# The last tile in two activations and two multiplies of 4 rows instead of four of 2

## The chip, the cores and the metric

The kernel runs on one core of a Trainium2 chip. The metric is the device time of one execution in microseconds (us). Where a profile is shown, its times count from the start of the span, which is some 2 us shorter than the device time (468.5 us in the profile of a run of 470.59).

## The reference, cut to what matters

```python
def reference(x):                     # x: (32, 512, 2048) float32
    x1, x2 = x[..., :1024], x[..., 1024:]
    return (x1 * (1 / (1 + np.exp(-x1)))) * x2      # silu(x1) * x2
```

The input is 134 MB, the output 67 MB. Each element is used once.

## The kernel before

The 16,384 rows are cut into 16 tiles of 128 partitions x 8 rows. There are two input and two output buffers. For each tile ScalarE (ACT) writes silu of the first half into the output buffer, and VectorE (DVE) multiplies it in place by the second half. Loads are issued from SyncE's queue, stores from ScalarE's. `silu` and `mul` below take a range of rows.

```python
    load(0)
    load(1)
    for i in range(n_tiles):
        ...
        if i < n_tiles - 1:
            kc = KC_EDGE if i == 0 else K           # 2 rows at a time in tile 0, else all 8
            for c in range(0, K, kc):
                silu(ot, xt, c, c + kc)
                mul(ot, xt, c, c + kc)
            for ps, ks in OPENING if i == 0 else [(slice(None), slice(None))]:
                nc.scalar.dma_start(out=ov[ps, ks], in_=ot[ps, ks])
            if i + 2 < n_tiles:
                load(i + 2)
            continue
        # the last tile
        for c in range(0, K, KC_EDGE):              # KC_EDGE = 2
            silu(ot, xt, c, c + KC_EDGE)
            if c == K - KC_EDGE:
                nc.scalar.dma_start(out=ov[:, :KS], in_=ot[:, :KS])    # KS = 4
            mul(ot, xt, c, c + KC_EDGE)
        nc.scalar.dma_start(out=ov[:, KS:], in_=ot[:, KS:])
```

## Time and profile before

| | before |
|---|---|
| time, first three runs | 470.60, 470.62, 472.49 us |
| span of the profiled run | 468.5 us |
| DVE busy, ACT busy | 30%, 24% |
| traffic | 201.3 MB, 430 GB/s over the span |
| last tile's work released | 447.89 us |
| its two stores issued | 454.36 and 458.76 us |
| landed | 462.4 and 467.5 us |

The way to read it is from the end. The last row sets the span. Whether the rows above it matter depends on whether the transfer queue had other bytes to move when each store was issued. The lines are shown with the prediction.

### The profile page before, as it was taken

What the parts mean: (1) busy time and instruction counts of PE and PEld (TensorE: products, weight loads), DVE (VectorE), ACT (ScalarE), POOL (GpSimd) and SP (SyncE); (2) the same over time, 40 slices, a digit from 0 to 9 for tenths busy, and PEclk for the clock granted to TensorE, in tenths of its full rate; (3) what the DMA queues carried; (4) which work ended last, traced back from release to release, by engine and by line L of the source; (5) the groups of instructions that cost most, each with busy time, mean ns of one, the idle gap of its engine ahead of it and who ended that gap; (6) DMA issues with size and microseconds to landing.
All of it is one profiled execution on the core that took longest, in us unless ns stands there. A gap on an engine that the chain in (4) does not pass through costs nothing.

```text
span 468.5 us, 189 instructions
## 1 busy us (share of the span) xinstructions
DVE 139.5 (30%) x22; ACT 114.3 (24%) x23; POOL 0.2 (0%) x4
## 2 busy tenths in 40 slices
DVE  0070600704207052070510606116060150602551
ACT  1142305005050140601406023060230603206060
POOL 0000000000000000000000000000000000000000
DMA  9999999999999999999999999899999899999998
GB/s 425 397 453 425 448 403 403 492 403 403 448 487 408 403 448 414 481 403 425 425 448 448 403 448 492 358 448 448 431 464 448 380 425 492 403 448 403 448 403 359
DMA packets 4881, 201.34 MB, mean 430 GB/s; under 512 B 592, under 2 KB 592, under 8 KB 592
## 3 DMA queue, kind: packets, MB, share of 16 engines
q1 hardware_dynamic: 2304, 134.22, 66.4%
q10 hardware_dynamic: 2576, 67.11, 33.2%
q14 instruction: 1, 0.01, 0.0%
HBM read 134.22 MB, written 67.11 MB: 430 GB/s over the span
## 4 chain that ended last, share of the span: by engine, by line
DMA 72%; DVE 14%; ACT 11%; DVEq 0%; issue 0%
DMA out_dram<-ot 63%; DVE ot L93 14%; ACT ot L86 11%; DMA xt<-in_x_dram 9%; DVEq L148 0%
## 5 line engine op out<-in xcount | busy, mean ns | idle before, releaser
L93 DVE TENSOR_TENSOR ot<-ot,xt 128x8192 f32<-128x8192 f32 (+1 forms) x22 | 139.5, 6363 | 319.2 <-ACT ot L86 319.2
L86 ACT ACTIVATE ot<-xt 128x8192 f32<-128x8192 f32 (+1 forms) x22 | 113.0, 5163 | 340.1 <-DMA out_dram<-ot 306.1
L86 ACT ACT_TABLE_LOAD x1 | 1.3, 1283 | 0.8 <-PEq L137 0.8
L137 POOL MEMSET const-bfloat16-1.0<- 128x1 bf16 x1 | 0.1, 103 | 0.0
L137 POOL MEMSET const-uint8-127<- 128x1 uint8 x1 | 0.1, 102 | 0.0
L137 POOL MEMSET const-float32-0.0<- 128x1 f32 x1 | 0.1, 100 | 0.2 <-issue 0.2
L137 POOL MEMSET const-float32-1.0<- 128x1 f32 x1 | 0.1, 99 | 0.0
## 6 DMA issues: line engine op xcount, KB each, us to landing
out_dram<-ot ACTq DMA_DIRECT2D x14, 4096.0 KB, 42.2
out_dram<-ot ACTq DMA_DIRECT2D x3, 2048.0 KB, 8.8
out_dram<-ot ACTq DMA_DIRECT2D x2, 512.0 KB, 17.1
out_dram<-ot ACTq DMA_DIRECT2D x1, 768.0 KB, 27.9
xt<-in_x_dram SPq DMA_DIRECT2D x16, 35.1
out_dram<-ot ACTq DMA_DIRECT2D x1, 256.0 KB, 10.8
```

What stands on the lines that cost most here:

```text
L86: nc.scalar.activation(out=ot[:, c:ce, :], in_=xt[:, c:ce, :half], func=mybir.ActivationFunctionType.Silu,)
L93: nc.vector.tensor_mul(out=ot[:, c:ce, :], in0=ot[:, c:ce, :], in1=xt[:, c:ce, half:],)
L137: nc = _bacc.Bacc("TRN2", target_bir_lowering=False, num_devices=1)
```

## The change

The intent is fewer instructions in the last tile, each with its fixed cost, and both stores issued after all of its compute instructions. The first tile's five growing stores, which the change's description also names, are in both kernels.

```diff
-        for c in range(0, K, KC_EDGE):
-            silu(ot, xt, c, c + KC_EDGE)
-            if c == K - KC_EDGE:
-                nc.scalar.dma_start(out=ov[:, :KS], in_=ot[:, :KS])
-            mul(ot, xt, c, c + KC_EDGE)
-        nc.scalar.dma_start(out=ov[:, KS:], in_=ot[:, KS:])
+        for c in range(0, K, KS):
+            silu(ot, xt, c, c + KS)
+            mul(ot, xt, c, c + KS)
+        for c in range(0, K, KS):
+            nc.scalar.dma_start(out=ov[:, c:c + KS], in_=ot[:, c:c + KS])
```

## The prediction

> **What bounds the kernel now.** I read the page first (busy shares, the row of slices, traffic), then the chain of waits in order of time, the timeline of the tail, the instruction groups by form, and last the transfers in short windows of the tail. From the page:
>
> ```profile
> DVE 139.5 (30%) x22; ACT 114.3 (24%) x23; POOL 0.2 (0%) x4
> ...
> DMA  9999999999999999999999999899999899999998
> ...
> HBM read 134.22 MB, written 67.11 MB: 430 GB/s over the span
> ```
>
> Both compute engines are idle for 70% of the span or more; the transfer engines are at nine tenths in nearly every slice. The kernel is bound by 201.3 MB of traffic, and the change leaves every byte of it. So only the tail can matter: what the end waits for once the last bytes cannot be kept queued. The last lines of the chain of waits (start, us, what):
>
> ```profile
> 410.49 37.38 DMA out_dram<-ot
> 447.87 0.02 issue
> 447.89 1.92 ACT ot L86
> 449.81 0.02 issue
> 449.83 6.70 DVE ot L93 x3
> 456.53 2.20 DVEq L148
> ```
>
> The reader should see that the last tile's first activation (447.89) is released not by its input but by the landing of the store of two tiles earlier, which frees the output buffer. The last line is misleading: the chain ends at 458.73 with the last multiply, yet the span is 468.5 us. The last 9.8 us, a store, are missing from it. So I take the end from transfers, not from this chain. The timeline of the tail (start, us, engine, line; ACTq rows are store issues):
>
> ```profile
> 439.47 0.34 ACTq L112 DMA_DIRECT2D out_dram<-ot  x1
> 447.89 7.31 ACT L86 ACTIVATE ot<-xt 128x2048 f32<-128x2048 f32 x4 [17.17 <-DMA out_dram<-ot]
> 449.83 8.90 DVE L93 TENSOR_TENSOR ot<-ot,xt 128x2048 f32<-128x2048 f32 x4 [10.39 <-ACT ot L86]
> 454.36 0.34 ACTq L120 DMA_DIRECT2D out_dram<-ot  x1
> 458.76 0.34 ACTq L122 DMA_DIRECT2D out_dram<-ot  x1
> ```
>
> The list of issues in narrow windows around these three gives their times to landing: 18.0, 8.0 and 8.8 us. They land therefore at 439.47 + 18.0 = 457.5, 454.36 + 8.0 = 462.4 and 458.76 + 8.8 = 467.5. The spacing is the argument: from 447.87 (the landing before them) to 457.5 is 9.6 us for 4 MiB, then 4.9 and 5.1 us for 2 MiB each, all between 410 and 437 GB/s. The store queue never runs dry after 447.9. It drains 8 MiB at the full rate, while the last tile is computed beside it. When do the first bytes of the last tile begin? In the window from 456.8 to 457.2 the transfer view has
>
> ```profile
> DMA packets 32, 0.26 MB, mean 656 GB/s; under 512 B 16, under 2 KB 16, under 8 KB 16
> ```
>
> which I read as sixteen tiny packets, the end marks of the previous store, one for each transfer engine, and sixteen data packets of 16 KiB (16 x 16,384 B = 0.26 MB), each engine's first of the last tile. So the first half, issued at 454.36, waits some 2.4 to 2.8 us behind older bytes. The window 461.65 to 462.1 shows the same count for the second half: issued at 458.76, it waits about 3 us. These two slacks are all that the change can eat.
>
> **What the Trainium skill says.** "DMA: Bandwidth & Descriptors", section "Queues, rings and completion order", says that each transfer engine takes the descriptors of one issuing queue in ring order; the handover at 457.0 agrees, with the new store's packets beginning beside the old one's end marks. The same page, "Latency and other measured facts", gives about 600 ns from issue to first byte for transfers issued as here. The trace has one issue into empty queues, the opening load at 0.00 us, and its first packets begin later than that: the windows from 0.5 to 2 us show no traffic before 1.0 and 1835 GB/s from 1.0 to 1.5. I use the trace's 1.0 to about 1.8 us, though as the first transfer of the program it may be slower than a later one. [...]
>
> **The change part by part.** The mean durations come from the groups by form:
>
> ```profile
> L93 DVE TENSOR_TENSOR ot<-ot,xt 128x8192 f32<-128x8192 f32 x14 | 121.7, 8693 | 285.0 <-ACT ot L86 285.0
> L86 ACT ACTIVATE ot<-xt 128x8192 f32<-128x8192 f32 x14 | 98.4, 7029 | 303.1 <-DMA out_dram<-ot 288.9 <-DMA xt<-in_x_dram 14.2
> L93 DVE TENSOR_TENSOR ot<-ot,xt 128x2048 f32<-128x2048 f32 x8 | 17.8, 2286 | 34.2 <-ACT ot L86 34.2
> L86 ACT ACTIVATE ot<-xt 128x2048 f32<-128x2048 f32 x8 | 14.6, 1897 | 37.0 <-DMA xt<-in_x_dram 19.8 <-DMA out_dram<-ot 17.2
> ```
>
> *Activations.* The slope is (7029 - 1897)/6144 = 0.835 ns per element, so one of 4096 takes 1897 + 2048 x 0.835 = 3.61 us. Two replace four: busy 7.2 against 7.6 us. They still begin at 447.89, since what frees the buffer is untouched.
>
> *Multiplies.* The slope is (8693 - 2286)/6144 = 1.043, so 4.42 us each; two for four is 8.84 against 9.14 us busy. Back to back they start 0.08 us early into each other in the trace (four take 8.90 us of wall time).
>
> *Pipeline fill.* This is the cost. The first multiply can begin only after 3.61 us of activation instead of 1.90, so 1.71 us later: 447.89 + 3.61 + 0.04 = 451.54. It ends at 455.96. The second activation ends at about 455.1, before that, so the second multiply follows directly and ends at 455.96 - 0.08 + 4.42 = 460.30.
>
> *Stores.* They keep their size and split, two of 2048 KB. Placing the first issue after both activations costs nothing, since it waits for the multiply anyway. They are issued at about 455.98 and 460.33 instead of 454.36 and 458.76: 1.6 us later each. The saved fixed costs (1.71 late at the start, 1.57 at the end) return only 0.14 us.
>
> *Does the delay reach the end?* First half: issue 455.98, plus 1.0 to 1.4 us for most engines by the opening load, gives first bytes at 457.0 to 457.4, the last perhaps 457.8. The old store's bytes end between 456.8 and 457.2. Engine by engine that is a gap of 0 to 0.6 us, about 0.2 us on average; with the skill's 0.6 us it would be none. Second half: issue 460.33, first bytes 461.3 to 462.1; the first half, itself 4.9 us of transfer, ends at about 461.9 to 462.5. No second gap. Of 1.6 us of delay, some 1.4 are thus absorbed by the queue, and the sum is +0.2 us, rounded, on 470.62: 470.8 us.
>
> **The rivals.** *The queue runs dry.* If issuing takes longer than in the opening, say 2.0 us, the first half starts a full 1 us late and the time is about 471.6. If nothing were hidden at all it would be 470.62 + 1.6 = 472.2, the most that the delay can cost. For it: the margin is under 1 us, and landings, not first bytes, end the program. Against it: the measured slack of 2.4 to 2.8 us. *Fewer instructions win.* The saved 0.4 us of activation and 0.3 us of multiply could show if compute set the end; the chain of waits, which ends in DVE, seems to say so. That would give 470.0 at best. Against it: the pipeline fill costs more than the saving, and the last 9.8 us hold no compute. *All hidden anyway.* With a latency under 0.9 us the transfers do not move, and the time stays at 470.6. This is the nearest rival, and I cannot exclude it from one opening load.
>
> **Range and chances.** The before runs are 470.60, 470.62 and 472.49, so one run in three lies 0.4% up without any change; I let the range reach 472.1 for this and for most of the dry queue, and down to 470.3 for ordinary scatter. Two per cent is 9.4 us, six times the largest delay, so I give 98% to within 2%, and 1% each to faster and slower.
>
> **What would show it.** Right: groups of 128x4096 at about 3.61 and 4.42 us; the first multiply at 451.5; issues at 456.0 and 460.3; time to landing of both halves shortened by about 1.4 us, to 6.6 and 7.4; landings within 0.3 us of 462.4 and 467.5; the transfer row at full rate across 457. Wrong: a hole of over 0.6 us in the transfers after 457, or the stores' time to landing unchanged at 8.0 and 8.8 (the delay passed on whole), or any movement before 447.9.

## The result, and the profile after

| | before | changed |
|---|---|---|
| median of 6 runs each | 471.23 us (470.60 to 472.49) | 470.35 us (470.27 to 471.34) |
| ratio | | 0.9981, 95% interval 0.9964 to 0.9999: the same |

A ratio is the mean time of one kernel's fast runs over that of the other's in the same rounds, so it is not quite the ratio of the medians quoted. The before runs fall in two groups, three at 470.6 to 470.8 and three at 471.6 to 472.5, and the median of six lies between them. This makes the first difference look larger than it is; the controls below put it at 0.2 us.

The page of the changed kernel answers the first lines shown of before:

```profile
DVE 139.3 (30%) x20; ACT 114.1 (24%) x21; POOL 0.2 (0%) x4
...
HBM read 134.22 MB, written 67.11 MB: 430 GB/s over the span
```

Two instructions are gone from each engine, 0.2 us of busy time each; traffic and rate are the same. The new forms in the groups by form (busy us, then mean ns, then idle before):

```profile
L93 DVE TENSOR_TENSOR ot<-ot,xt 128x4096 f32<-128x4096 f32 x2 | 8.8, 4422 | 12.1 <-ACT ot L86 12.1
L86 ACT ACTIVATE ot<-xt 128x4096 f32<-128x4096 f32 x2 | 7.1, 3608 | 17.2 <-DMA out_dram<-ot 17.2
```

The timeline of the tail (start, us, engine, line):

```profile
439.57 0.34 ACTq L112 DMA_DIRECT2D out_dram<-ot  x1
448.01 7.12 ACT L86 ACTIVATE ot<-xt 128x4096 f32<-128x4096 f32 x2 [17.20 <-DMA out_dram<-ot]
451.66 8.76 DVE L93 TENSOR_TENSOR ot<-ot,xt 128x4096 f32<-128x4096 f32 x2 [12.13 <-ACT ot L86]
456.12 4.67 ACTq L120 DMA_DIRECT2D out_dram<-ot  x2
```

The last row merges the two store issues; the second starts at 456.12 + 4.67 - 0.34 = 460.45. The list of issues gives 6.4 and 6.9 us to landing, so they land at 462.5 and 467.4. The stores are issued 1.7 to 1.8 us later than before and land within 0.1 us of the same times: the delay was taken out of their wait in the queue. In the transfer view of 456.8 to 457.3 us the handover from tile 14's store is where it was, with all sixteen end marks and each engine's first 16 KiB of the last tile:

```profile
DMA packets 32, 0.26 MB, mean 524 GB/s; under 512 B 16, under 2 KB 16, under 8 KB 16
```

The chain of waits again ends in VectorE, with the last multiply:

```profile
448.01 3.62 ACT ot L86
451.64 0.02 issue
451.66 4.42 DVE ot L93
456.09 4.34 DVEq L146
```

That chain now ends at 460.43, 1.7 us later than the 458.73 of before, yet the span is not longer. So this end of the chain is no measure of the end of the program.

To compare tails, I count from the release of the last tile (its first activation's start) to the last landing: 467.51 - 447.89 = 19.62 us before and 467.38 - 448.01 = 19.36 us after (landings from the trace's records). The tail is 0.26 us shorter. Merging work that begins later should not do this, and the experiments look for it. One line differs in the transfer view. Between 463 and 464.2 us, inside its last store, the kernel before has

```profile
q10 hardware_dynamic: 30, 0.49, 96.0%
q14 instruction: 1, 0.01, 1.6%
```

(queue, kind, packets, MB, share of the 16 engines), one fetch of instructions, 8,192 B and 0.31 us on one transfer engine. The changed kernel has no instruction packet between the release and the last landing; the only one after the release stands in the trace at 469.02, after the end of the span (the kernel before has a second one there too, at 470.33). From 447.9 to 468 us its transfer view lists one queue:

```profile
q10 hardware_dynamic: 416, 7.86, 91.4%
```

The landings tell the same. A store lands in 16 parts, one for each transfer engine. In the kernel before, fifteen parts of the last store had landed 19.36 us after the release, no later than all sixteen of the changed kernel, and one came 0.26 us after them. The records don't say which engine the fetch ran on.

### The profile page after: what moved, and what is told of

It is laid out like the page before. It is cut to its first block, busy times and chain, and to the rows that moved or that the text cites. A ratio compares the mean times of both kernels' runs of the same rounds, so it can differ in the third digit from the quotient of the medians.

```text
span 468.4 us, 185 instructions
## 1 busy us (share of the span) xinstructions
DVE 139.3 (30%) x20; ACT 114.1 (24%) x21; POOL 0.2 (0%) x4
## 4 chain that ended last, share of the span: by engine, by line
DMA 72%; DVE 14%; ACT 11%; DVEq 1%; issue 0%
DMA out_dram<-ot 63%; DVE ot L93 14%; ACT ot L86 11%; DMA xt<-in_x_dram 9%; DVEq L146 1%
## 5 line engine op out<-in xcount | busy, mean ns | idle before, releaser
L93 DVE TENSOR_TENSOR ot<-ot,xt 128x8192 f32<-128x8192 f32 (+2 forms) x20 | 139.3, 6983 | 321.1 <-ACT ot L86 321.1
L86 ACT ACTIVATE ot<-xt 128x8192 f32<-128x8192 f32 (+2 forms) x20 | 112.8, 5661 | 340.2 <-DMA out_dram<-ot 305.8
```

The source lines that it names most:

```text
L86: nc.scalar.activation(out=ot[:, c:ce, :], in_=xt[:, c:ce, :half], func=mybir.ActivationFunctionType.Silu,)
L93: nc.vector.tensor_mul(out=ot[:, c:ce, :], in0=ot[:, c:ce, :], in1=xt[:, c:ce, half:],)
```

## The experiments

Two theories are to be told apart, for two different things. For the 1.7 us that vanished, **queue**: a store's delay costs nothing until its first bytes would come after the last bytes of the store ahead of it, and from there costs its full length. The rival is **compute**: the last multiply sets the end. For the 0.26 us that was won, **fetch**: the instruction fetch of 0.31 us fell out of the last store. The rival is that the merged tail itself gains, or that it is chance. Twelve kernels ran, all correct, each timed in 5 rounds beside the kernel before. Kernels of one set share its rounds: the first four, the next four and the last four. The sets ran on three different chips, where the kernel before had medians of 470.52, 470.58 and 470.64 us, so a tenth between sets says nothing. The edits are shown shortened, and are against the changed kernel unless said otherwise.

**1. The kernel before again** (no edit).

> The kernel before, unedited, as a control. It tells whether the difference of 0.19% (ratio 0.9981) is in the kernels or in the sample. Chance theory: its ratio to before lies in the same few tenths of a per cent, with an interval that holds 1. Fetch theory (an instruction fetch of 8 KB and 0.31 us fell into the last store of the kernel before at 463.6 us, and not into that of the changed kernel): the instruction row of the DMA queues shows one packet inside the span again and the last landing is again about 0.3 us later, counted from the release of the last tile, than in the changed kernel.

470.52 us median (470.35 to 471.57), ratio 0.9998 (0.9985 to 1.0012); the kernel before had 470.52 over 9 runs in these rounds. The profile fell on the run of 471.57. In it the last tile was released at 449.23 instead of 447.89, so the 1.3 us of that slower run arose upstream of everything that the change touches. The trace's end marks of tile 14's store show one transfer engine 1.2 us or more behind the fastest (456.82 to 458.51, against 456.83 to 457.17 in the first profile). The fetch was there again, at 464.86, but the tail was 19.36 us long. The expected 0.3 us did not show: the engine that was already behind set the end. The last parts of its three stores landed at 458.87, 463.76 and 468.60, 4.89 and 4.84 us apart; so the fetch did not delay that engine, and the other fifteen were done 1.0 us before it.

**2. The changed kernel again** (no edit).

> The changed kernel, unedited, as the other control. Queue theory: the same end, 0 to 0.3 us from before, ratio 0.9985 to 1.0005. Fetch theory: ratio 0.9993 or below (0.3 us or more faster), and no instruction packet within the last store. Compute theory (the last multiply sets the end): 1.6 us slower, ratio 1.003, which the first result already speaks against.

470.31 us median, all five runs within 470.29 to 470.44; ratio 0.9991 (0.9978 to 1.0003). The tail was 19.33 us and no fetch lay in it. The gain is 0.2 us against the median of before, and the interval still holds 1. The compute theory's 1.6 us is excluded.

**3. Only the multiplies merged.**

```diff
-            silu(ot, xt, c, c + KS)      # c = 0, 4
+            silu(ot, xt, c, c + 2)
+            silu(ot, xt, c + 2, c + 4)
             mul(ot, xt, c, c + KS)
```

> Only the multiplies of the last tile are merged (four activations of 2 rows, two multiplies of 4). The first multiply starts after two activations, about 3.7 us after the release, so the stores are issued some 1.6 us later than before, as in the changed kernel. Queue theory: nothing at the end, 470.2 to 470.7 us. Compute theory: +1.6 us. Fetch theory: if the fetch belongs to VectorE's instructions it vanishes here as in the changed kernel; if to ScalarE's it stays and the time is that of before.

**4. Only the activations merged.**

```diff
             silu(ot, xt, c, c + KS)      # c = 0, 4
-            mul(ot, xt, c, c + KS)
+            mul(ot, xt, c, c + 2)
+            mul(ot, xt, c + 2, c + 4)
```

> Only the activations of the last tile are merged (two activations of 4 rows, four multiplies of 2). The first multiply starts 1.7 us later than before, stores at about 456.0 and 460.4. Queue theory: nothing at the end, 470.2 to 470.7 us. Compute theory: +1.6 us. Fetch theory: if the fetch belongs to ScalarE's instructions it vanishes here as in the changed kernel; if to VectorE's it stays and the time is that of before.

470.94 us (470.90 to 471.04) and 471.04 us (470.92 to 471.29), both above the range that I gave the queue theory, and both slower than the fully merged tail (at most 470.44) in the same rounds. Yet their stores are issued at the same moments: 456.10 and 456.13 against 456.12 in the first profile of the changed kernel, and their first halves land at 462.5. Only the second half is late, with 7.5 us to landing in both instead of 6.9. In both, the transfer view from 462.6 to 468.5 us has the fetch, at 465.9 in the trace:

```profile
q14 instruction: 1, 0.01, 0.3%
```

So merging either half alone did not remove the fetch. At first this speaks against a fetch that belongs to one engine, for each kernel shares one engine's compute instructions with the changed one. The number of records may resolve it (a record is any instruction, wait or store issue that the trace lists for an engine). ScalarE's queue has 66 records in the kernel before, 64 in the changed one, and 66 in *both* of these: in kernel 3 because it keeps four activations, in kernel 4 because each of its two stores has come to wait on ScalarE as well as VectorE, which adds two waits. VectorE has 58 in kernel 3 and 60 in kernel 4. The number that goes with the fetch is ScalarE's. A second packet goes with VectorE's in the same way: all five profiles with 60 VectorE records, and none of the eight with 58, have one 1.8 us after the end of the span, where it delays nothing.

**5. Pieces of one row** (eight activations and eight multiplies, same stores).

```diff
-        for c in range(0, K, KS):
-            silu(ot, xt, c, c + KS)
-            mul(ot, xt, c, c + KS)
+        for c in range(K):
+            silu(ot, xt, c, c + 1)
+            mul(ot, xt, c, c + 1)
```

> The last tile in activations and multiplies of 1 row, same two stores. Fill is shorter: first store issued at about 453.6 us, some 0.8 us earlier than before and 2.4 us earlier than the changed kernel. Queue theory: no gain, since the first half still waits for the older bytes until about 457.0: 470.2 to 470.7 us, with times to landing longer by what the issue is earlier. Compute theory: the last multiply ends at about 458 us, so about 0.7 us faster than before.

471.47 us median, but from 470.25 to 472.51: too scattered to time a few tenths. Its profile is of a run released late, at 449.32. The first store was issued 5.75 us after the release, against 6.47 before and 8.11 changed; its first half took 8.8 us to landing; and the tail was 19.38 us. With issues up to 2.4 us apart, the tails are 19.38 here, 19.36 in the control of before and 19.36 and 19.33 in the changed kernel: issuing earlier gains nothing.

**6 to 8. The first activation made longer**: 5 and 3 rows, 6 and 2, and one of 8, with multiplies of 4 as in the changed kernel.

```diff
-        for c in range(0, K, KS):
-            silu(ot, xt, c, c + KS)
-            mul(ot, xt, c, c + KS)
+        silu(ot, xt, 0, 5)               # 6 in the next kernel, 8 (and no second) in the last
+        mul(ot, xt, 0, 4)
+        silu(ot, xt, 5, 8)
+        mul(ot, xt, 4, 8)
```

> The changed kernel with activations of 5 and 3 rows instead of 4 and 4. Activation of 5 rows 4.46 us, first store issued at about 456.9 to 457.0, 0.85 us later than in the changed kernel; second at 461.3. Queue theory with the 0.85 us from issue to first byte that the changed kernel's trace shows: first bytes at about 457.8, the queue dry for some 0.8 us, time about 0.7 to 0.9 us above the changed kernel (471.1). With the 1.0 to 1.8 us of the prediction: 1.0 to 1.4 above. All hidden: nothing.

> Activations of 6 and 2 rows. First activation 5.32 us, first store issued at about 457.8, 1.7 us later than in the changed kernel. Queue theory: first bytes at about 458.6, dry for 1.6 us, time 1.5 to 1.8 us above the changed kernel (472.0), of which the second store adds nothing. If a dry queue cost a restart of its own, more than that, by the same amount at 5, 6 and 8 rows.

> One activation of 8 rows, two multiplies of 4. First store issued at about 459.5, 3.4 us later than in the changed kernel. Queue theory: dry for some 3.3 us, time 3.2 to 3.5 us above the changed kernel (473.7): past the knee every us of delay costs a us. A queue that hides more than the trace shows would give less than 3 us.

| | issue of first store after release | its first bytes after issue | tail | median |
|---|---|---|---|---|
| changed kernel | 8.11 us | 0.85 us | 19.36 us | 470.35 |
| 5 and 3 rows | 8.96 | 0.84 | 20.17 | 471.06 (lowest 470.95) |
| 6 and 2 rows | 9.81 | 0.84 | 21.02 | 472.52 (lowest 471.86) |
| 8 rows | 11.52 | 0.84 | 22.73 | 473.81 (lowest 473.70) |

The medians are less sure than the tails here: on this chip each of the three kernels had one to three runs a microsecond or more above its lowest, and the median of 6 and 2 rows missed the expected 472.0. The lowest times (470.27 for the changed kernel) rise by 0.68, 1.59 and 3.43 us.

The hole opens as the queue theory says. The transfer engines in the windows of the kernel with 6 and 2 rows (window, its length, busy DVE, ACT and POOL, clock, DMA share, GB/s):

```profile
457.30:457.75 0.45, 0.45 (x2) 0.00 (x0) 0.00 (x0) 1.00 0.00 0
457.75:458.55 0.80, 0.80 (x1) 0.00 (x0) 0.00 (x0) 1.00 0.00 0
458.55:460.34 1.79, 1.79 (x1) 0.00 (x0) 0.00 (x0) 1.00 1.05 439
```

and in the same windows of the changed kernel:

```profile
457.30:457.75 0.45, 0.45 (x1) 0.00 (x0) 0.00 (x0) 1.00 1.02 437
457.75:458.55 0.80, 0.80 (x1) 0.00 (x0) 0.00 (x0) 1.00 0.98 410
458.55:460.34 1.79, 1.79 (x1) 0.00 (x0) 0.00 (x0) 1.00 1.03 439
```

With 6 and 2 rows nothing moves until 458.55, then the rate is the full one at once. Past the changed kernel, the tail grows by 0.81, 1.66 and 3.37 us for issues that are 0.85, 1.70 and 3.41 us later. This is one for one, with no extra cost of restarting. In all four, the tail is the time of the first bytes plus 10.4 us (changed: 8.11 + 0.85 + 10.40 = 19.36). Before the knee (the delay at which the slack is used up) the slope is zero: 6.47 and 8.11 us give the same first bytes, 8.95 us after the release.

The changed kernel thus stands almost exactly on the knee. Its first bytes (from 456.97) begin 0.1 us after the first end marks of the older store (from 456.85). The whole slack has been spent.

**9 to 12. The number of ScalarE's instructions alone**, changed at tile 6, far from the tail. The first is the changed kernel with

```diff
-                silu(ot, xt, 0, 8)               # tile 6 only
+                silu(ot, xt, 0, 4)
+                silu(ot, xt, 4, 6)
+                silu(ot, xt, 6, 8)
```

> The changed kernel, with two more ScalarE instructions far from the tail: the activation of tile 6 in pieces of 4, 2 and 2 rows. ScalarE's records in the trace go from 64 to 66, the number of all four kernels that had an instruction fetch in the last store. Fetch theory (ScalarE's instruction stream crosses a block): one instruction packet inside the last store again, and the end 0.3 to 0.7 us later than the changed kernel: 470.6 to 471.0 us. If the merged tail itself is what gains or the two merged-half kernels lost by their own schedule: no packet, or a packet and 470.3 us.

470.85 us; four of five runs at 470.81 to 470.92, against 470.29 to 470.44 for the changed kernel in the first set. ScalarE has 66 records, and the transfer view from 462.6 to 468.5 us has the packet again:

```profile
q10 hardware_dynamic: 167, 2.23, 89.3%
q14 instruction: 1, 0.01, 0.3%
```

The profile is of the fifth run, 472.18, released 1.3 us late; counted from the release, its tail is 19.96 us, 0.6 longer than the changed kernel's, with an identical tail in the source. (One transfer engine was late in this run too, and here it did not hide the fetch.) The late engine had been caught up by then: the first half's last two parts landed 0.1 us apart, and of the last store's sixteen parts fifteen had landed 19.36 us after the release. The expectation of the fetch theory is met in all three: packet, tail, time. The time alone would not carry it, as the next kernel shows.

The control has two more multiplies instead:

```diff
-                mul(ot, xt, 0, 8)                # tile 6 only
+                mul(ot, xt, 0, 4)
+                mul(ot, xt, 4, 6)
+                mul(ot, xt, 6, 8)
```

> The changed kernel, with two more VectorE instructions: the multiply of tile 6 in pieces of 4, 2 and 2 rows. Control for the one before. Fetch theory with ScalarE: no instruction packet in the last store, 470.3 us as the changed kernel. If it were VectorE's fetch or any extra instruction: the packet and 470.6 to 471.0 us.

No packet in the last store, as expected, and a tail of 19.48 us. The time missed, at 470.72 us (470.61 to 471.88). The control was not clean: ScalarE has 65 records, one wait more. The span ends 1.25 us after the last landing, where the changed kernel needs 1.01, and ScalarE's closing drain takes 132 ns instead of 8. A fetch that now falls due in the closing instructions would explain this, but the trace has no packet inside the span to show it (its next fetch is at 469.12, 0.33 us after the end), so it stays open. The two padded kernels thus differ by 0.13 us in median time and by 0.48 us in the tail: what sets them apart is the packet and the tail, not the time. Of the 0.4 us that this control lost against the changed kernel's first profile, 0.24 lie after the last landing and 0.12 in the tail.

The other two have tile 6's activation in eight pieces of 1 row, in the changed kernel and in the kernel before:

```diff
-                silu(ot, xt, 0, 8)               # tile 6 only
+                for c in range(8):
+                    silu(ot, xt, c, c + 1)
```

> The changed kernel, with seven more ScalarE instructions: the activation of tile 6 in eight pieces of 1 row. Fetch theory: the block is crossed earlier, before the last tile's stores (at about 440 to 452 us, as in the kernel with pieces of 1 row), where the delay of one transfer engine is spread or still carried on: 470.3 to 470.7 us.

> The kernel before with its tail of 2-row pieces unchanged, and the same seven more ScalarE instructions at tile 6. Fetch theory: the fetch leaves the last store, and the kernel before ends as early as the changed one, 470.3 us, although it has more instructions, not fewer. If instead the merged tail is what gains: 470.5 to 470.6 us, as the kernel before.

The fetch moved to 449.6 and 449.7 us, as foreseen. The changed kernel so padded took 470.47 us (470.31 to 470.60), with a tail of 19.50. The kernel before so padded took 470.59 (470.51 to 471.83), with a tail of 19.60: no gain at all over the 470.64 of before in these rounds. My expectation of 470.3 failed. The reason can be read one landing earlier. Tile 14's store landed 9.84 and 9.92 us after the release in these two, 9.61 to 9.66 in all the other profiles. The fetch costs 0.2 to 0.3 us there and the delay is still mostly present at the end. My reading is that it is not enough that the fetch leaves the last store: it must come after the last byte, as it does with 64 records. That was not tested with the kernel before, of which no version with fewer ScalarE records was run.

| kernel | ScalarE records | fetch at | tail |
|---|---|---|---|
| first activation of 8 rows | 63 | 1.0 us after the span | 22.73 us (queue dry) |
| changed, twice | 64 | 0.6 us after the span | 19.36, 19.33 |
| 5 and 3 rows, 6 and 2 rows | 64 | 0.6 us after the span | 20.17, 21.02 (queue dry) |
| changed + 2 multiplies | 65 | 0.3 us after the span | 19.48 |
| before, twice | 66 | 463.6, 464.9 | 19.62, 19.36 (late engine) |
| one half merged, two kernels | 66 | 465.9 | 20.07, 20.10 |
| changed + 2 activations | 66 | 467.1 | 19.96 |
| pieces of one row | 70 | 450.9 | 19.38 (late engine) |
| changed + 7, before + 7 | 71, 73 | 449.6, 449.7 | 19.50, 19.60 |

## Why the prediction was right, and where its sizes were off

*The bound and the method were right.* The end was a matter of transfers, and reading it from landings instead of the chain of waits was what kept a compute delay of 1.7 us from being taken for a loss. The chain moved by 1.7 us and the span did not.

*Durations.* 3.61 us became 3608 ns and 4.42 us became 4422 ns. The delay of the stores, counted from the release, was 8.11 - 6.47 = 1.64 us, against the 1.6 worked out.

*The step that was mis-sized* is "issue 455.98, plus 1.0 to 1.4 us for most engines by the opening load". The time from issue to first bytes was 0.84 to 0.85 us in ten profiles where the queue was empty or just emptying (the three longer first activations show it cleanest). The program's first transfer was slower and did not represent a later one. The slack that the prediction read as 2.4 to 2.8 us runs to the first bytes; less the 0.84 us it is about 1.6, and the delay of 1.64 just used it up. The term "+0.2 us" was therefore about zero, and the rival "All hidden anyway", with its "latency under 0.9 us", is what happened to the delay. The predicted 6.6 and 7.4 us to landing were 6.4 and 6.9.

*What was not in the working* is the fetch. In the profile on which every number was built, one of sixteen parts of the last store landed 0.26 us after the rest, with the fetch beside it; without the fetch the predicted +0.2 became about -0.2 us. In the rounds of the two controls that is 470.52 against 470.31. That adding two ScalarE instructions far upstream brings the fetch back into the last store, with a tail 0.6 us longer, is shown, in one profile. That the fetch is the whole of the 0.2 us is argued: the padded kernel before gained nothing, and the multiply control lost 0.4 us with no fetch inside its span. That crossing an instruction block is what triggers it is inferred from the counts. How much one fetch costs is not settled: tails grew by nothing (twice) to 0.7 us, and why 0.7 where it comes at 465.9 but 0.26 at 463.6 stays open.

*The rival "Fewer instructions win"* is right in sign by accident. Fewer instructions did win a little, but not through their busy time: the multiplies end 1.7 us later. With only one half of the merging, half of the saving in compute instructions came with a loss of 0.4 to 0.5 us.

*The range* held, with the median of 470.35 at its lower end of 470.3. That is partly luck: the lower end was set for ordinary scatter, not for a gain, and a step that the prediction did not know took the time there. The tail of slower runs (471.3 to 472.5) occurs in both kernels; in the slower runs that were profiled the last tile was already released 1.3 to 1.4 us late.

No version beat the changed kernel's median: earlier issue gains nothing, later issue loses, and what remains is 201.3 MB at the rate at which it moves.

## What to carry to other kernels

In these runs a later store was free as long as its first bytes were ready before the queue ahead of it had drained, and then cost one for one. The slack can be read as the time from issue to landing minus what the same store takes into an empty queue (here 8.0 - 6.3 = 1.7 us, and 1.64 us of delay used it up), and not from a chain that ends at the last compute instruction. When a change of a few instructions moves the time of a transfer-bound kernel by some tenths of a microsecond, look for other packets in the transfer queues, such as instruction fetches, before crediting the change. Vary a suspected delay in several steps across the knee: one step short of it says nothing about where it is.

## What the Trainium skill lacked or had wrong

- "DMA: Bandwidth & Descriptors", section "Latency and other measured facts", gives about 600 ns to the first byte for transfers issued as here, and does not say from where it counts. These runs show 0.84 to 0.85 us from the start of a store's issue to its first packet in an empty queue (0.50 us from the end of the issuing instruction, which takes 0.34), and 1.0 us from the start of the issue of the program's first load.
- "Runtime: NRT & Kernel Launch", section "Instruction fetch mechanics", says that a sequencer fetches its next instructions through its own DMA queue and that the cost is "mostly hidden". The runs agree on a queue of its own, but where the page has refills in blocks of 16 KiB the packets here are 8,192 B, and beside saturated transfers the fetch is not free: 0.31 us on one transfer engine. Of eight tails that held it, six were 0.1 to 0.7 us longer than the changed kernel's and two were not.
- No page that I read says that an added semaphore wait (kernel 4, two more ScalarE records) counts toward the instructions that bring a fetch on, as the 66 records with the fetch in its last store suggest.
